# A decoder layer in float32r parts: all first-query-tile scores in parts, and attention inserted in fewer, larger pieces

## The chip, the cores and the metric

The kernel runs on one core of one Trainium2 chip. The metric is device time in microseconds (us) of one execution; three executions of the kernel before took 318.89, 319.07 and 320.75, so its time is the median, 319.07.

## What is computed

One layer for 256 tokens of width 1024. A combined projection gives queries, keys and values for two groups of heads; differential attention (four heads, two softmaxes each, subtracted) and causal attention (eight heads of 64) run on them; an output projection, LayerNorm, a SwiGLU network and a second LayerNorm follow. Cut to what matters:

```
proj = x @ w_in                       # dq dk dv mq mk mv, 512 columns each; rope on q and k
s = q @ k.T * 64**-0.5;  s = where(kpos <= qpos, s, -inf)
a = softmax(s_0) - lam * softmax(s_1)     # group A, 4 heads: 8 score matrices
o_A = rmsnorm(a @ v) * g * (1 - lambda_init)
o_B = softmax(s) @ v                      # group B, 8 heads (256 tokens are one block)
x = layer_norm(ALPHA * x + concat(o_A, o_B) @ w_o)
x = layer_norm(ALPHA * x + (silu(x @ w_g) * (x @ w_u)) @ w_f2)
```

## The kernel before, in words

All weights arrive in units of 128 x 4 x 512 float32 (`raw`). Each unit is split exactly into two float32r parts: `hi` is a cast on ScalarE (L96), `lo` is `raw - hi` on VectorE (L98), with one piece in four of the units 2 to 9 on GpSimd. A product is then three matmuls, hi*hi + hi*lo + lo*hi (`mm3`, L131 to L134). Ring buffers hold five raw units and four of each part.

The input projection has six chunks of 512 columns. Chunks 0 to 3 are q and k of group A, then q and k of group B, each transposed (`proj_qkT`, 32 steps of three matmuls of 256 columns); chunks 4 and 5 are the values of both groups (`proj_v`, 16 steps of three matmuls of 512 columns). Attention is woven in: a table says at which step of which chunk a piece of attention stands in TensorE's program (L38 to L40). `rope` takes a finished block of q or k out of PSUM: a shuffle (`sh`) and a product (`a`) on VectorE, a product on GpSimd, then `finish`: the sum (`a`, L241), a cast to `h` (L243, ScalarE), `l = a - h` (L244, VectorE), and `f` (L245, ScalarE), the first 128 tokens in plain float32.

`scores(g, j)` (L258) makes the scores of two heads: per head three float32r matmuls for query tile 1 (128 queries, 256 keys) from `h` and `l`, and one plain float32 matmul for query tile 0 (128 keys) from `f`. VectorE then adds the mask and takes the row minimum of the negated scores (L271, two instructions per head, each with a read of its accumulator), and ScalarE takes the exponential with its row sum (L274). The score tiles, the transposes of P and the PV products share a PSUM pool of four buffers (`psB`); a tile can be written when the reader of the tile four allocations earlier is done.

For group A, `diff_combine` (L288) subtracts the second softmax from the first on VectorE, after the last exponential of the group; `diff_pt(h)` (L299) transposes the result of one head (three 128x128 transposes, `ppd`, L279 to L281). For group B, `norm1` (L444) and `moba_norm` scale P and `moba_pt` transposes it (`ppm`). `diff_pv` and `moba_pv` multiply by V, and the output projection `wo` follows.

Which instruction of an engine stands where is decided by a list scheduler of the framework from these insertion steps; every engine then runs its own list strictly in order, except that TensorE may load weights ahead.

Of the kernel before, what the change touches and what calls it, by code (L numbers as in the profile page):

```python
# [11 lines left out]
F32 = mybir.dt.float32  # L12
# [18 lines left out]
WARM = 7  # matmuls on zeros that raise the tensor engine's clock while the first loads run  # L31

# weight units loaded / split in more pieces than usual: unit -> pieces
# [3 lines left out]
# steps of a projection chunk at which attention work is woven in  # L37
FIN0, FIN1, FIN2, FIN3 = (20, 24, 28, 31), (4, 6, 8, 10), (5, 4), (5, 2)  # L38
SCORES0, SCORES1 = (18, 22, 26, 30), (3, 5, 7, 9)
COMBINE, DIFF_PT = 12, (22, 25, 28, 31)  # L40

# partner of each rotary dim within a 32-partition quadrant
# [3 lines left out]
# The 256 tokens are one key block of the block-sparse group: there is no past block to select, so  # L46
# its softmax runs over the own block under the causal mask.
# Weight products: every float32 operand is split exactly into two float32r parts (12 bits each), and
# hi*hi + hi*lo + lo*hi accumulate in PSUM.
# [3 lines left out]
def hybrid_layer_kernel(ctx, tc, xT, xr, w_in, w_o, w_f1, w_f2, cols, rows, lamb, rot, tri, out):  # L53
# [11 lines left out]
    # unit: [128, 4 blocks, 512] float32, split into two float32r parts  # L65
# [39 lines left out]
    def spread(units_, pieces, steps):  # L105
        """Hooks that emit the split of some units evenly over a number of steps."""
# [101 lines left out]
    apool = axT.enter_context(tc.tile_pool(name="apool", bufs=1))  # L208
    V = [apool.tile([P, 2, 512], F32, name=f"V{i}") for i in range(2)]
    # per pair of 128-row blocks: first token tile in float32, the rest in two float32r parts  # L210
    F0, QH, QL, SH, QA = {}, {}, {}, {}, {}

    def qk_tiles(c, b):
        kind = c % 2
        n = S if kind else P
        F0[c, b] = apool.tile([P, 2, P], F32, tag=f"f{kind}{b}", name=f"f{c}_{b}")
        QH[c, b] = apool.tile([P, 2, n], F32R, tag=f"h{kind}{b}", name=f"h{c}_{b}")
        QL[c, b] = apool.tile([P, 2, n], F32R, tag=f"l{kind}{b}", name=f"l{c}_{b}")
# [7 lines left out]
    def rope(c, js, ps):  # L226
        """128-row blocks js of q^T or k^T, PSUM -> SBUF, with the rotary part applied."""
# [10 lines left out]
        f, h, l = F0[c, b][:, bs, :], QH[c, b][:, bs, :], QL[c, b][:, bs, :]  # L238

        def finish():  # L240
            nc.vector.tensor_add(a, a, sh)  # L241
            src = a if c % 2 else a[:, :, P:]
            nc.scalar.copy(h, src)  # L243
            nc.vector.tensor_sub(l, src, h.bitcast(F32))  # L244
            nc.scalar.copy(f, a[:, :, :P])  # L245
# [12 lines left out]
    def scores(g, j):  # L258
        b, i = divmod(j, 2)
        cq, ck = 2 * g, 2 * g + 1  # L260
        pr = [psB.tile([P, 3 * P], F32, tag="b", name=f"s{g}_{j}_{s}") for s in range(2)]
        for s in range(2):
            r = slice(64 * s, 64 * s + 64)
            mm3(pr[s][:, :S], QH[cq, b][r, i, :], QL[cq, b][r, i, :], QH[ck, b][r, i, :], QL[ck, b][r, i, :], True, True)
        for s in range(2):
            r = slice(64 * s, 64 * s + 64)
            nc.tensor.matmul(pr[s][:, S:], F0[cq, b][r, i, :], F0[ck, b][r, i, :], start=True, stop=True)
        for s in range(2):
            u = 2 * j + s
            for i, (e, p, m) in enumerate(((E0[g][:, u, :], pr[s][:, S:], mask[:, P:]), (E1[g][:, u, :], pr[s][:, :S], mask))):  # L270
                nc.vector.tensor_tensor_reduce(  # L271
                    out=e, in0=p, in1=m, scale=-0.125, scalar=3.4e38, op0=ALU.add, op1=ALU.min,
                    accum_out=negm[g][:, i, u : u + 1])
                nc.scalar.activation(e, e, AF.Exp, bias=negm[g][:, i, u : u + 1], scale=-1.0,  # L274
                                     accum_out=ls[g][:, i, u : u + 1])
# [12 lines left out]
    def diff_combine():  # L288
        """E_c0 - lam * (l0 / l1) * E_c1, per query row."""
# [84 lines left out]
    def proj_qkT(c, side):  # L374
        """One 512-column chunk, transposed: 128 columns on the partitions, 256 tokens."""
# [29 lines left out]
    def proj_v(c, side):  # L405
        """One 512-column chunk for both token tiles."""
# [18 lines left out]
    for j in range(4):  # L425
        sc.setdefault(SCORES0[j], []).append(lambda j=j: scores(0, j))
# [3 lines left out]
    for h in range(4):  # L430
        sc.setdefault(DIFF_PT[h], []).append(lambda h=h: diff_pt(h))
# [3 lines left out]
    for j in range(4):  # L435
        sc.setdefault(SCORES1[j], []).append(lambda j=j: scores(1, j))
# [11 lines left out]
    for n, u in enumerate(range(6)):  # L448
        sd.setdefault(8 + n, []).append(lambda u=u: moba_pt(u))
    proj_v(5, sd)  # L450

# [93 lines left out]
    ahead(15)  # L545
    mp.close()

# [1 line left out]
    hp = ctx.enter_context(tc.tile_pool(name="hp", bufs=1))  # L549
    hTh = hp.tile([P, NF, S], F32R, name="hTh")  # L550
    hTl = hp.tile([P, NF, S], F32R, name="hTl")
# [176 lines left out]
```

## Time and profile before

| | us | of the span |
|---|---|---|
| time, median of three | 319.07 | |
| span of the profiled execution | 317.0 | |
| TensorE (PE) busy | 304.6 | 96% |
| TensorE weight loads (PEld) busy | 259.7 | 82% |
| VectorE (DVE) busy | 224.4 | 71% |
| ScalarE (ACT) busy | 169.0 | 53% |
| GpSimd (POOL) busy | 36.1 | 11% |
| granted TensorE clock, mean | 0.993 | |

The profiled execution's own time inside the records is its span, 317.0 us; the median of the timed runs is 2.07 us more. The shares are means over stages with different limits: attention is woven into the first third only, and the last two thirds are the feed-forward network, in which TensorE runs without a gap. In the trace a matmul's start is the useful number: ends are modelled, so neighbours overlap, and the distance between starts is what a matmul costs.

### The profile page before, as it was taken

What the parts mean: (1) busy time and instruction counts of PE and PEld (TensorE: products, weight loads), DVE (VectorE), ACT (ScalarE), POOL (GpSimd) and SP (SyncE); (2) the same over time, 40 slices, a digit from 0 to 9 for tenths busy, and PEclk for the clock granted to TensorE, in tenths of its full rate; (3) what the DMA queues carried; (4) which work ended last, traced back from release to release, by engine and by line L of the source; (5) the groups of instructions that cost most, each with busy time, mean ns of one, the idle gap of its engine ahead of it and who ended that gap; (6) DMA issues with size and microseconds to landing.
All of it is one profiled execution on the core that took longest, in us unless ns stands there. A gap on an engine that the chain in (4) does not pass through costs nothing.

```text
span 317.0 us, 4689 instructions
## 1 busy us (share of the span) xinstructions
PE 304.6 (96%) x1741; PEld 259.7 (82%) x1741; DVE 224.4 (71%) x437; ACT 169.0 (53%) x349; POOL 36.1 (11%) x38
## 2 busy tenths in 40 slices
PE   7999899999999999999999999999999999999990
PEld 4999789867887788888888888888888888888880
DVE  3799999999977389949386577658657753343275
ACT  3757489398685328247467547646754642422000
POOL 1076553310030010100000000000000000000011
PEclk9999999999999999999999999999999999999997
DMA  6999963444376442659654574475357474000011
GB/s 176 377 305 375 423 236 134 132 135 147 125 254 213 188 136 74 212 247 309 220 172 142 218 254 136 142 267 167 141 224 254 144 266 132 0 2 0 0 66 67
DMA packets 12310, 57.18 MB, mean 180 GB/s; under 512 B 1504, under 2 KB 2272, under 8 KB 6784
## 3 DMA queue, kind: packets, MB, share of 16 engines
q1 hardware_dynamic: 12000, 54.79, 49.5%
q0 software_dynamic: 288, 2.10, 1.9%
q8 instruction: 13, 0.21, 0.3%
q14 instruction: 9, 0.07, 0.1%
HBM read 55.84 MB, written 1.05 MB: 179 GB/s over the span
## 4 chain that ended last, share of the span: by engine, by line
PE 77%; DVE 12%; DMA 4%; issue 3%; POOL 1%; ACT 1%; SPq 1%; DVEq 0%; ACTq 0%
PE fc L590 21%; PE fc L591 11%; PE fo L134 6%; PE fo L132 6%; PE fo L133 6%; DMA raw<-in_w_in_dram 4%; DVE lo L98 4%; PE wo L132 2%; PE fr L133 2%; PE fr L132 2%; PE wo L134 2%; PE wo L133 2%; PE fr L134 2%; PE pj L132 2%; PE pj L134 2%
## 5 line engine op out<-in xcount | busy, mean ns | idle before, releaser
L98 DVE TENSOR_TENSOR lo<-raw,hi 128x1024 fp32r<-128x1024 f32 (+1 forms) x122 | 118.2, 995 | 41.2 <-ACT hi L96 41.1
L96 ACT CAST hi<-raw 128x512 fp32r<-128x512 f32 (+1 forms) x130 | 100.5, 824 | 38.3 <-PE fo L134 19.2
L590 PE MATMUL fc<-x1T,hi 128*128 128x512 f32 x288 | 100.1, 392 | 0.0
L591 PE MATMUL fc<-x1T,lo 128*128 128x256 f32 x288 | 80.7, 280 | 0.0
L590 PEld LDWEIGHTS fc<-x1T,hi 128*128 128x128 f32 x288 | 54.1, 188 | 11.8
L591 PEld LDWEIGHTS fc<-x1T,lo 128*128 128x128 f32 x288 | 54.1, 188 | 0.0
L132 PE MATMUL pj<-xTh,hi 128*128 128x256 f32 x128 | 37.1, 296 | 1.0 <-DVE xTh L168 0.9
L134 PE MATMUL pj<-xTh,lo 128*128 128x256 f32 x128 | 36.2, 289 | 0.7 <-DVE lo L98 0.5
L133 PE MATMUL pj<-xTl,hi 128*128 128x256 f32 x128 | 36.6, 287 | 0.0
L132 PE MATMUL fo<-hi,hTh 128*128 128x512 f32 x82 | 32.4, 395 | 0.0
L133 PE MATMUL fo<-lo,hTh 128*128 128x512 f32 x82 | 32.4, 395 | 0.0
L134 PE MATMUL fo<-hi,hTl 128*128 128x512 f32 x82 | 32.4, 395 | 0.0
L132 PEld LDWEIGHTS pj<-xTh,hi 128*128 128x128 f32 x128 | 24.6, 195 | 2.6 <-ACT hi L180 2.1
L134 PEld LDWEIGHTS pj<-xTh,lo 128*128 128x128 f32 x128 | 24.4, 194 | 1.3 <-DVE lo L98 0.7
L594 DVE TENSOR_TENSOR v<-v,fc 128x256 f32<-128x256 f32 x36 | 15.0, 418 | 14.5 <-ACT v L593 14.5
L133 PEld LDWEIGHTS pj<-xTl,hi 128*128 128x128 f32 x128 | 25.0, 195 | 0.0
L593 ACT COPY v<-fc 128x256 f32<-128x256 f32 x36 | 13.3, 370 | 20.8 <-PE fc L591 20.7
L505 POOL TENSOR_TENSOR rsf<-rsf,mhalf 128x1 f32<-128x1 f32 x2 | 1.8, 924 | 179.3 <-DVE rsf L504 179.3
L134 PEld LDWEIGHTS fo<-hi,hTl 128*128 128x128 f32 x82 | 15.5, 189 | 3.6
L133 PEld LDWEIGHTS fo<-lo,hTh 128*128 128x128 f32 x82 | 15.5, 189 | 3.6
L132 PEld LDWEIGHTS fo<-hi,hTh 128*128 128x128 f32 x82 | 15.5, 189 | 3.5
L98 POOL TENSOR_TENSOR lo<-raw,hi 128x512 fp32r<-128x512 f32 x8 | 13.5, 1689 | 21.3 <-ACT hi L96 21.3
(148 smaller groups left out, 455.8 us busy)
## 6 DMA issues: line engine op xcount, KB each, us to landing
raw<-in_w_f_dram SPq DMA_DIRECT2D x33, 1024.0 KB, 5.2
raw<-in_w_in_dram SPq DMA_DIRECT2D x24, 256.0 KB, 5.4
raw<-in_w_in_dram SPq DMA_DIRECT2D x4, 1024.0 KB, 10.1
raw<-in_w_o_dram SPq DMA_DIRECT2D x4, 1024.0 KB, 4.8
raw<-in_w_in_dram SPq DMA_DIRECT2D x4, 512.0 KB, 7.9
rows<-in_rows_dram POOLq DMA_DIRECT2D x2, 1024.0 KB, 6.9
x_sb<-in_xr_dram SPq DMA_DIRECT2D x1, 1024.0 KB, 10.5
out_dram<-z SPq DMA_DIRECT2D x3, 256.0 KB, 2.1
```

Source lines behind the costliest of these rows:

```text
L96: nc.scalar.copy(h[:, s, :], r[:, s, :])
L98: eng.tensor_sub(l[:, s, :], r[:, s, :], h[:, s, :].bitcast(F32))
L132: nc.tensor.matmul(ps, sh, mh, start=first, stop=False)
L133: nc.tensor.matmul(ps, sh, ml, start=False, stop=False)
L134: nc.tensor.matmul(ps, sl, mh, start=False, stop=last)
L505: nc.gpsimd.tensor_tensor(rs, rs, mhalf[:, :1], op=ALU.pow)
L590: nc.tensor.matmul(ps, hi[u][:, i, ws], x1T[:, k], start=k == 0, stop=False)
L591: nc.tensor.matmul(ps[:, 0, :], lo[u][:, i, ws], x1T[:, k, 0, :], start=False, stop=k == KT - 1)
L593: nc.scalar.copy(v, ps[:, 1, :])
L594: nc.vector.tensor_add(v, v, ps[:, 0, :])
```

## The change

Six things change together.

- `rope` no longer makes `f`; `h` and `l` of the queries cover all 256 tokens instead of the last 128 (keys had all 256 already).
- Query tile 0's scores are three float32r matmuls of 128 columns from `h` and `l`, like tile 1's, instead of one plain float32 matmul.
- `scores(g, b)` handles four heads, and so takes all four `psB` buffers at once; the two heads of a pair alternate matmul by matmul.
- The insertion steps change from four per group to two: `SCORES0` (18, 22, 26, 30) to (20, 30), `SCORES1` (3, 5, 7, 9) to (5, 11).
- `diff_combine` stands at step 14 of chunk 3 instead of 12, and the transposes of group A at steps 25 and 31, two heads at a time, instead of 22, 25, 28, 31.
- `moba_pt` likewise: two heads at steps 8, 10 and 12 of chunk 5, instead of one at each of 8 to 13.

```diff
-SCORES0, SCORES1 = (18, 22, 26, 30), (3, 5, 7, 9)
-COMBINE, DIFF_PT = 12, (22, 25, 28, 31)
+SCORES0, SCORES1 = (20, 30), (5, 11)
+COMBINE, DIFF_PT = 14, (25, 31)
...
         def finish():
             nc.vector.tensor_add(a, a, sh)
-            src = a if c % 2 else a[:, :, P:]
-            nc.scalar.copy(h, src)
-            nc.vector.tensor_sub(l, src, h.bitcast(F32))
-            nc.scalar.copy(f, a[:, :, :P])
+            nc.scalar.copy(h, a)
+            nc.vector.tensor_sub(l, a, h.bitcast(F32))
...
+    def scores(g, b):
+        cq, ck = 2 * g, 2 * g + 1
+        pr = {}
+        for i in range(2):
+            for s in range(2):
+                pr[i, s] = psB.tile([P, 3 * P], F32, tag="b", name=f"s{g}_{b}_{i}_{s}")
+            for q, o, n in ((slice(P, S), 0, S), (slice(0, P), S, P)):
+                for p, (A, B) in enumerate(((QH, QH), (QL, QH), (QH, QL))):
+                    for s in range(2):
+                        r = slice(64 * s, 64 * s + 64)
+                        nc.tensor.matmul(pr[i, s][:, o : o + n], A[cq, b][r, i, q], B[ck, b][r, i, :n],
+                                         start=p == 0, stop=p == 2)
...
-    for j in range(4):
-        sc.setdefault(SCORES0[j], []).append(lambda j=j: scores(0, j))
+    for b in range(2):
+        sc.setdefault(SCORES0[b], []).append(lambda b=b: scores(0, b))
...
-        sc.setdefault(DIFF_PT[h], []).append(lambda h=h: diff_pt(h))
+        sc.setdefault(DIFF_PT[h // 2], []).append(lambda h=h: diff_pt(h))
...
-    for n, u in enumerate(range(6)):
-        sd.setdefault(8 + n, []).append(lambda u=u: moba_pt(u))
+    for u in range(6):
+        sd.setdefault(8 + 2 * (u // 2), []).append(lambda u=u: moba_pt(u))
```

The scheduler reorders VectorE's list as well. The first place is ahead of group A's combine, in chunk 3 (`lo` with `raw`, `hi`: a weight piece; `sc`: the combine's factors; `E`: the exponentials that it combines). Before:

```order
L271 ISA negm_516 128x1
L235 STREAM_SHUFFLE sh_1_744<-pj_1_520 128x512
L236 TENSOR_TENSOR a_1_745<-pj_1_520,cs_sb 128x512
L98 TENSOR_TENSOR lo_754<-raw_521,hi_753 128x512
L241 TENSOR_TENSOR a_1_745<-a_1_745,sh_1_744 128x512
L291 RECIPROCAL rl_518<-ls_517 128x16
L292 TENSOR_TENSOR sc<-ls_517,rl_518 128x8
L98 TENSOR_TENSOR lo_754<-raw_521,hi_753 128x512
L244 TENSOR_TENSOR l_1_743<-a_1_745,h_1_742 128x256
L293 TENSOR_SCALAR sc<-sc,nlam 128x8
L98 TENSOR_TENSOR lo_754<-raw_521,hi_753 128x512
L296 SCALAR_TENSOR_TENSOR E_514<-E_514,sc 128x128
```

The same place now:

```order
L272 ISA negm_508 128x1
L233 STREAM_SHUFFLE sh_1_745<-pj_1_512 128x512
L234 TENSOR_TENSOR a_1_746<-pj_1_512,cs_sb 128x512
L98 TENSOR_TENSOR lo_822<-raw_596,hi_821 128x512
L239 TENSOR_TENSOR a_1_746<-a_1_746,sh_1_745 128x512
L292 RECIPROCAL rl_510<-ls_509 128x16
L98 TENSOR_TENSOR lo_822<-raw_596,hi_821 128x512
L293 TENSOR_TENSOR sc<-ls_509,rl_510 128x8
L98 TENSOR_TENSOR lo_822<-raw_596,hi_821 128x512
L241 TENSOR_TENSOR l_1_744<-a_1_746,h_1_743 128x512
L294 TENSOR_SCALAR sc<-sc,nlam 128x8
L297 SCALAR_TENSOR_TENSOR E_506<-E_506,sc 128x128
```

The count of `lo` rows shown is three in both, but they are of unit 8 before and of unit 9 now: unit 8's three stand further up now, between the score reductions, so that three more `lo` pieces of VectorE's come before the combine in all; and `l` has 512 columns instead of 256.

The second place is on VectorE from group B's first finished key block (`l_0`) to its first score reduction (`E` with `s`), chunks 3 and 4. Before:

```order
L244 TENSOR_TENSOR l_0_833<-a_0_835,h_0_832 128x512
L235 STREAM_SHUFFLE sh_1_926<-pj_1_750 128x512
L236 TENSOR_TENSOR a_1_927<-pj_1_750,cs_sb 128x512
L98 TENSOR_TENSOR lo_941<-raw_751,hi_940 128x512
L241 TENSOR_TENSOR a_1_927<-a_1_927,sh_1_926 128x512
L98 TENSOR_TENSOR lo_941<-raw_751,hi_940 128x512
L271 ISA E_931,negm_933<-s_0_0_959,mask 128x128
```

The same stretch now:

```order
L239 TENSOR_TENSOR a_0_834<-a_0_834,sh_0_833 128x512
L241 TENSOR_TENSOR l_0_832<-a_0_834,h_0_831 128x512
L98 TENSOR_TENSOR lo_938<-raw_752,hi_937 128x512 x3
L233 STREAM_SHUFFLE sh_1_923<-pj_1_751 128x512
L234 TENSOR_TENSOR a_1_924<-pj_1_751,cs_sb 128x512
L98 TENSOR_TENSOR lo_938<-raw_752,hi_937 128x512
L239 TENSOR_TENSOR a_1_924<-a_1_924,sh_1_923 128x512
L98 TENSOR_TENSOR lo_1016<-raw_838,hi_1015 128x512 x2
L241 TENSOR_TENSOR l_1_922<-a_1_924,h_1_921 128x512
L98 TENSOR_TENSOR lo_1016<-raw_838,hi_1015 128x512 x2
L272 ISA E_928,negm_930<-s_0_0_0_963,mask 128x128
```

Over the whole list up to that first reduction there are five more `lo` pieces than before, and one more `l` (the second key block's, which stood behind the first head's reductions). `l_0` now stands directly behind the sum `a_0` from which ScalarE makes its `h`.

## Rows read from the trace of the kernel before

**Rows 1.** Stretches: length, busy PE, PEld, DVE, ACT, POOL, then clock, DMA, GB/s.
```profile
50.00:66.00 16.00, 15.05 (x118) 13.79 (x117) 15.97 (x31) 10.40 (x28) 5.75 (x4) 1.00 0.39 124
66.00:80.00 14.00, 13.95 (x78) 10.46 (x77) 13.54 (x49) 12.92 (x44) 1.30 (x1) 1.00 0.45 159
80.00:100.00 20.00, 20.00 (x120) 16.59 (x119) 17.76 (x36) 13.64 (x34) 2.79 (x2) 1.00 0.55 188
```

**Rows 2.** Chain of waits around 57 us: start, us, what.
```profile
54.43 0.60 DVE lo L98
...
57.84 0.33 PE ppd L280
58.28 0.12 PE pj L132
```

**Rows 3.** Timeline of TensorE, one insertion of scores: start, us, engine, line, operation.
```profile
41.38 0.28 PE L134 MATMUL pj<-xTh,lo 128*128 128x256 f32 x1
41.59 0.39 PE L132 MATMUL s<-h,h 64*128 64x256 f32 x2
...
42.05 0.39 PE L267 MATMUL s<-f,f 64*128 64x128 f32 x4
42.37 0.39 PE L132 MATMUL pj<-xTh,hi 128*128 128x256 f32 x1
42.59 0.28 PE L133 MATMUL pj<-xTl,hi 128*128 128x256 f32 x1
```

**Rows 4.** Timeline of TensorE's weight loads in that insertion.
```profile
41.59 0.19 PEld L132 LDWEIGHTS s<-h,h 64*128 64x128 f32 x2
41.70 0.20 PEld L133 LDWEIGHTS s<-l,h 64*128 64x128 f32 x2
```

**Rows 5.** Instructions grouped by line and form: busy, mean ns, idle before.
```profile
L244 DVE TENSOR_TENSOR l<-a,h 128x256 fp32r<-128x256 f32 x6 | 2.3, 414 | 0.0
...
L244 DVE TENSOR_TENSOR l<-a,h 128x512 fp32r<-128x512 f32 x2 | 1.4, 677 | 0.0
L243 ACT CAST h<-a 128x512 fp32r<-128x512 f32 x2 | 1.2, 624 | 2.5 <-DVE a L241 2.5
...
L244 DVE TENSOR_TENSOR l<-a,h 128x128 fp32r<-128x128 f32 x4 | 1.0, 278 | 0.0
```

**Rows 6.** Timeline of TensorE in chunk 4, and at `wo`.
```profile
64.27 0.39 PE L133 MATMUL pj<-lo,xTh 128*128 128x512 f32 x1
64.50 0.40 PE L134 MATMUL pj<-hi,xTl 128*128 128x512 f32 x1
...
74.53 0.40 PE L133 MATMUL pj<-lo,xTh 128*128 128x512 f32 x1
...
96.33 0.39 PE L134 MATMUL wo<-hi,mixl 128*128 128x512 f32 x1
```

**Rows 7.** Timeline of VectorE: score reductions, combine, second group, `mixl`.
```profile
43.19 0.27 DVE L271 CUSTOM_DVE_ANT_0 E<-s,mask 128x128 f32<-128x128 f32 x1
...
43.74 0.28 DVE L271 CUSTOM_DVE_ANT_0 E<-s,mask 128x128 f32<-128x128 f32 x1
...
56.02 3.73 DVE L296 SCALAR_TENSOR_TENSOR E<-E,sc 128x128 f32<-128x128 f32 x8
...
69.20 0.28 DVE L271 CUSTOM_DVE_ANT_0 E<-s,mask 128x128 f32<-128x128 f32 x1
...
78.36 0.25 DVE L444 RECIPROCAL rl<-ls 128x16 f32<-128x16 f32 x1 [0.43 <-ACT E L274]
...
94.09 0.74 DVE L333 SCALAR_TENSOR_TENSOR mixl<-dm,gsub,mixh 128x512 fp32r<-128x512 f32 x1
```

**Rows 8.** Timeline of ScalarE: the exponentials of one head, and the next head's first.
```profile
50.33 0.39 ACT L274 ACTIVATE E<-E,negm 128x128 f32<-128x128 f32 x1
...
51.20 0.39 ACT L274 ACTIVATE E<-E,negm 128x128 f32<-128x128 f32 x1
```

**Rows 9.** A stretch behind the last matmul, columns as in Rows 1.
```profile
311.00:313.00 2.00, 0.00 (x0) 0.00 (x0) 2.00 (x5) 0.00 (x0) 0.46 (x1) 0.90 0.00 0
```

More of the change, by code (lines that the diff above doesn't have):

```diff
@@ L209, in hybrid_layer_kernel @@
     V = [apool.tile([P, 2, 512], F32, name=f"V{i}") for i in range(2)]
-    F0, QH, QL, SH, QA = {}, {}, {}, {}, {}
+    QH, QL, SH, QA = {}, {}, {}, {}
     def qk_tiles(c, b):
         kind = c % 2
[L215 to L218, printed above, removed]
+        QH[c, b] = apool.tile([P, 2, S], F32R, tag=f"h{kind}{b}", name=f"h{c}_{b}")
+        QL[c, b] = apool.tile([P, 2, S], F32R, tag=f"l{kind}{b}", name=f"l{c}_{b}")
     epool = axT.enter_context(tc.tile_pool(name="epool", bufs=1))
@@ L237, in rope @@
         nc.gpsimd.tensor_mul(sh, sh, sin2[:, :m, :])
-        f, h, l = F0[c, b][:, bs, :], QH[c, b][:, bs, :], QL[c, b][:, bs, :]
+        h, l = QH[c, b][:, bs, :], QL[c, b][:, bs, :]
         def finish():
             nc.vector.tensor_add(a, a, sh)
-            src = a if c % 2 else a[:, :, P:]
-            nc.scalar.copy(h, src)
-            nc.vector.tensor_sub(l, src, h.bitcast(F32))
-            nc.scalar.copy(f, a[:, :, :P])
+            nc.scalar.copy(h, a)
+            nc.vector.tensor_sub(l, a, h.bitcast(F32))
         return finish
@@ L256, in alloc_group @@
         rl[g] = small.tile([P, 2, 8], F32, tag="rl", name=f"rl{g}")
-    def scores(g, j):
-        b, i = divmod(j, 2)
+    def scores(g, b):
         cq, ck = 2 * g, 2 * g + 1
[L261 to L275, printed above, removed]
+        pr = {}
[8 more added lines that the diff above has]
+                                         start=p == 0, stop=p == 2)
+        for i in range(2):
+            for s in range(2):
+                u = 4 * b + 2 * i + s
+                for t, (e, p, m) in enumerate(((E0[g][:, u, :], pr[i, s][:, S:], mask[:, P:]),
+                                               (E1[g][:, u, :], pr[i, s][:, :S], mask))):
+                    nc.vector.tensor_tensor_reduce(
+                        out=e, in0=p, in1=m, scale=-0.125, scalar=3.4e38, op0=ALU.add, op1=ALU.min,
+                        accum_out=negm[g][:, t, u : u + 1])
+                    nc.scalar.activation(e, e, AF.Exp, bias=negm[g][:, t, u : u + 1], scale=-1.0,
+                                         accum_out=ls[g][:, t, u : u + 1])
@@ L434, in hybrid_layer_kernel @@
     sc = {FIN3[1]: fin}
-    for j in range(4):
-        sc.setdefault(SCORES1[j], []).append(lambda j=j: scores(1, j))
+    for b in range(2):
+        sc.setdefault(SCORES1[b], []).append(lambda b=b: scores(1, b))
     proj_v(4, sc)
```

## The prediction

> **What bounds the kernel now.** Read the stretches first [rows 1]: from 80 us on TensorE is busy in every microsecond (20.00 of 20.00, and so on to the end of the feed-forward network), so a delay of TensorE that is there at 80 us is still there at the end. Before 66 us VectorE has no room: 15.97 of 16.00 us busy from 50 to 66, 13.54 of 14.00 from 66 to 80. Then the chain of waits [rows 2]: up to 57.84 us it runs through VectorE (weight pieces, the combine of group A), and at 57.84 it passes to TensorE, at the second transpose of the first head, which needs the combined exponentials; from there it is TensorE's matmuls. So two questions decide: when will VectorE have combined the first head, and what does TensorE lose or gain between there and the end of the second group's scores.
>
> **An insertion of scores on TensorE.** Where it met no wait, the last projection matmul ahead started at 41.38 and the second one behind at 42.59 [rows 3]. Two projection matmuls at 0.12 each [rows 2] would have taken 0.24 of these 1.21 us, so an insertion for two heads costs 0.97. Its weight loads start 0.11 apart for both heads at once [rows 4]; five such slots (three of 256 columns, two of the plain float32 matmul) are 0.55, and the other 0.42 is the change from the full array to half the rows and back.
>
> After, a pair of heads has six slots, three of them with 128 columns. Their price isn't in the trace: no float32r matmul here has fewer than 256 columns. It is not below half the 0.12 of 256 columns, 0.06; and it could be as much as the plain float32 product of the same columns took, two instructions per head from 42.05 to 42.37 [rows 3], 0.32, less about 0.10 for the change back, 0.22. I take 0.11, because weight loads never start closer, so that a shorter matmul waits for the next load. An insertion of four heads is then 0.42 + 12 x 0.11 = 1.74.
>
> The Trainium skill (TensorE: Matmul & The Clock Gate, Back-to-back issue gap) gives about 81 ns per matmul of 128 columns with its load, in a stream. By that figure an insertion would cost an estimated 0.42 + 6 x 0.11 + 6 x 0.08 = 1.56, and the sum below would be lower by 3 x 0.03 = 0.1 us, since only the last three slots of one insertion lie on its path. No run here shows such a matmul yet.
>
> Group B's four insertions before, with their waits: from 64.50 to 74.53 [rows 6], 10.03 us, of which 20 projection matmuls at 0.23 [rows 6] are 4.62; so 5.41. Two new ones without a wait are 3.48. That is a gain of 1.93 for TensorE, if nothing else waits.
>
> Transposes two heads at a time: the six transposes cost the same; ScalarE's twelve copies remain. I cost this at nothing, between a gain of 0.1 and a loss of 0.1 for each joined pair (the 0.10 at a change of insertion above). The `f` copies that go were ScalarE's and not on the chain; what they give back there is in the waits below.
>
> **VectorE up to the combine.** The same list, plus: four `l` of 128 columns become 256, 4 x (414 - 278) ns = 0.54 us, and two of 256 become 512, 2 x (677 - 414) = 0.53 [rows 5]; together 1.07. Three more weight pieces now stand ahead of the combine, at 0.60 each [rows 2]: 1.80. VectorE was full, so the first head's combine is done 2.87 later: 57.84 becomes 60.71. What covers this on TensorE: the transposes stand three steps later, 9 matmuls, 9 x 0.12 = 1.08 us of work that moves from behind the wait to ahead of it. And the second head's transposes now follow at once: VectorE needs (59.75 - 57.84) / 3 = 0.64 per further head (59.75 is the end of the eight combines that start at 56.02 [rows 7]), TensorE needs only the two transposes left, 0.22; a wait of 0.4. The matmul that started at 64.50 starts at 64.50 + 2.87 - 1.08 + 0.4 = 66.69, **2.2 later**. What TensorE saves in group A's insertions (before 57 us) only makes it wait longer here.
>
> **Group B's scores.** Without new waits 2.2 - 1.93 = 0.3 would be left. But four heads take all four `psB` buffers, and the second insertion can't begin its last pair until VectorE has reduced the fourth head of the first. VectorE's first reduction of this group was at 69.20 [rows 7]. Ahead of it come now the 1.07, the second key block's `l` (0.68), and five weight pieces (3.00): 74.0. At 0.55 per head (43.19 to 43.74 [rows 7]) the fourth buffer is free at 76.2; six slots (0.66) and the change back (half the 0.42, 0.2) bring the matmul behind it to 77.0. Before, step 11 started five matmuls behind 74.53, at 75.69. So this wait leaves **1.3**, not 0.3.
>
> To that come pauses of VectorE that the old list hid. `l_0` stands directly behind the sum, and waits for ScalarE's cast, 0.62 [rows 5]; before, weight pieces lay between. In group A the fifth head's reductions stand behind pieces of unit 8, whose casts now queue behind four heads of exponentials: ScalarE needs 0.87 per head (50.33 to 51.20 [rows 8]), VectorE 0.55, so after four heads ScalarE is 4 x 0.32 = 1.3 late, which two ready pieces (1.2) nearly cover, but not the cast behind them, about 0.5. With GpSimd's part of `rope`, which the new list also has closer behind, these are between 0 and 2.0 us; I take half, 1.0, since some were there before in other places.
>
> **Sum.** 317.0 + 1.3 + 1.0 = 319.3 us of span. The median of the runs is 2.07 above the span, so **321.4 us**.
>
> **Behind it.** After group B's scores ScalarE has 16 heads' halves, 8 x 0.87 = 7.0 us of exponentials, in one run, and VectorE waits for the last before the reciprocal: from 75.2 (74.0, half a head, the 1.0) to 82.2 instead of 78.36 [rows 7], 3.8 later. From there to `mixl`, done at 94.83 [rows 7], VectorE has the same work as before, and TensorE took `mixl` at 96.33 [rows 6], 1.5 later. 3.8 - 1.5 is 2.3, exactly the delay already counted; so this costs nothing in the sum, and what is worse than the sum ahead of it comes out here one for one.
>
> **Bounds.** Low: VectorE's work up to the reciprocal is 1.07 more whatever the order, it had at most the 0.46 of pauses [rows 1] to fill, and TensorE has 1.5 of slack at `mixl`; so the best is 1.07 - 1.5 = -0.4, 318.7 us. High: all the pauses (2.0) and the dear matmul (3 x 0.11) are 1.3 + 2.0 + 0.3 = 3.6, 322.7 us.
>
> **Rivals.**
> - *The weight pieces moved, but TensorE takes the slack.* VectorE's list is the same length in the end (the pieces that come earlier are missing later), so if the pauses stay out and the 1.5 at `mixl` takes up the rest, the shift is -0.4 to 1.2: 318.7 to 320.3, middle 319.4. Against it: the fourth buffer at 76.2, which is counted without any pause. Chance 0.24.
> - *Slower by over 1%.* The place is the first pair of transposes. TensorE arrives there, by the buffers of group A, some 2 to 3 us ahead of VectorE. If that idle time is long enough for the granted clock to fall to 1.2 GHz, the projection behind it runs at half speed; four microseconds of it cost 2, and the time is 321.4 + 2 = 323.4. All pauses together give 322.7 without it. It decides from 0.9 us above the sum. For it: behind the last matmul, with TensorE quite idle, the mean is down to 0.90 from 311 to 313 [rows 9], so idleness does lower it; against it: here TensorE is busy up to the wait and right behind it. Chance 0.25, both mechanisms.
>   The Trainium skill (TensorE: Matmul & The Clock Gate, Part 1) says that half rate is the state to which idleness brings the array back, and activity releases it; the trace agrees [rows 9], and this rule speaks against joining waits into one long one.
> - *Faster by over 1%.* The waits inside the eight old insertions and the changes of array shape go and nothing replaces them: group B's 1.93, and as much again in group A, 3.9; 317.0 - 3.9 + 2.07 = 315.2. It needs VectorE to have room before 57 us, where it has 0.03 of 16 us [rows 1]. Chance 0.03.
>
> **How the numbers follow.** The forecast (shift 1.3 to 3.1, 320.4 to 322.2) has the remaining 0.48. About 1% (3.2 us) is what a measurement of this kernel tells from no change; 322.26 is that line. Faster 0.03; the forecast and the first rival, 0.72, are within 1% except for the forecast's last edge, 0.03: same 0.69; slower 0.28. The range leaves out the faster case, the lowest part of the first rival and the clock case's far end: 318.8 to 323.6.
>
> **What would show it.** In the changed profile: the first transpose of group A released by the combine at 60 to 62 us, with one idle time of 2 to 4 us ahead of it on TensorE; the first reduction of group B at 74 to 76; the reciprocal behind it waiting for an exponential; weight loads of the 128-column scores 0.11 apart; and the last third of the program shifted as a whole. It would be wrong if TensorE's wait at the transposes is under 1 us (VectorE had room after all), or if the clock falls there.

## The result, and the profile after

The changed kernel takes 324.66 us (median of four, 324.42 to 324.92); the kernel before, run beside it, 319.91. The ratio is 1.0164, 95% interval 1.0128 to 1.0200: slower by 1.6%, and 1.06 us above the upper end of the range. The span of the profiled execution is 322.6 us, 5.6 more than before, and the median is again 2.06 above the span. In some executions the granted clock falls to 0.50 between 10 and 16 us, which costs about 1.5 us: the profiled ones of e4, e10 and e13 show it, and of the four times of the kernel before, two (320.75, 320.87) lie about that much above the others (318.89, 319.07), so the 5.6 us between the spans say more of the change than the 4.75 between the medians.

The stretches of the changed kernel, columns as in [rows 1]:

```profile
42.00:44.00 2.00, 1.90 (x13) 1.79 (x14) 2.00 (x7) 1.16 (x3) 0.00 (x0) 0.60 0.65 270
...
60.00:62.00 2.00, 0.10 (x1) 0.00 (x0) 2.00 (x5) 0.62 (x1) 0.16 (x1) 1.00 0.00 0
62.00:64.00 2.00, 0.72 (x3) 0.51 (x4) 1.97 (x7) 0.00 (x0) 0.00 (x0) 0.72 0.34 74
64.00:66.00 2.00, 2.00 (x11) 1.84 (x10) 2.00 (x7) 0.96 (x2) 0.00 (x0) 0.50 1.00 426
...
50.00:66.00 16.00, 12.82 (x99) 12.18 (x97) 15.02 (x41) 9.94 (x31) 4.22 (x3) 0.90 0.54 195
66.00:80.00 14.00, 13.49 (x93) 11.01 (x92) 12.36 (x32) 7.94 (x21) 2.59 (x2) 0.99 0.30 95
```

TensorE is idle for 3 us around 60 to 63, and behind it the clock is at 0.50, the lower of its two levels. VectorE, which had 0.03 us of room from 50 to 66 and 0.46 from 66 to 80 [rows 1], now has 0.98 and 1.64: its milestones come later although it is less busy, so it waits. Where it waits, and when its milestones come, is in its timeline:

```profile
35.52 0.91 DVE L241 TENSOR_TENSOR l<-a,h 128x256 fp32r<-128x256 f32 x1
38.94 1.49 DVE L239 TENSOR_TENSOR a<-a,sh 128x256 f32<-128x256 f32 x1
...
46.04 0.69 DVE L239 TENSOR_TENSOR a<-a,sh 128x512 f32<-128x512 f32 x1 [0.69 <-POOL sh L235]
...
51.14 0.69 DVE L98 TENSOR_TENSOR lo<-raw,hi 128x512 fp32r<-128x512 f32 x1 [0.59 <-ACT hi L96]
52.18 1.36 DVE L98 TENSOR_TENSOR lo<-raw,hi 128x512 fp32r<-128x512 f32 x1 [0.35 <-ACT hi L96]
...
62.87 1.41 DVE L297 SCALAR_TENSOR_TENSOR E<-E,sc 128x128 f32<-128x128 f32 x4
...
67.72 0.69 DVE L239 TENSOR_TENSOR a<-a,sh 128x512 f32<-128x512 f32 x1 [0.90 <-POOL sh L235]
69.15 0.69 DVE L241 TENSOR_TENSOR l<-a,h 128x512 fp32r<-128x512 f32 x1 [0.74 <-ACT h L240]
...
77.84 0.28 DVE L272 CUSTOM_DVE_ANT_0 E<-s,mask 128x128 f32<-128x128 f32 x1
...
85.38 0.25 DVE L445 RECIPROCAL rl<-ls 128x16 f32<-128x16 f32 x1 [2.43 <-ACT E L275]
...
101.14 0.74 DVE L334 SCALAR_TENSOR_TENSOR mixl<-dm,gsub,mixh 128x512 fp32r<-128x512 f32 x1
```

Against [rows 7]: the combine starts at 62.87 instead of 56.02, group B's first reduction at 77.84 instead of 69.20 (8.64 later), the reciprocal at 85.38 instead of 78.36, `mixl` at 101.14 instead of 94.09. TensorE's timeline at the same places:

```profile
63.28 0.47 PE L280 MATMUL ppd<-ident,E 128*128 128x128 f32 x1 [3.18 <-DVE E L297]
...
71.90 0.40 PE L134 MATMUL pj<-hi,xTl 128*128 128x512 f32 x1
...
72.69 0.23 PE L265 MATMUL s<-h,h 64*128 64x128 f32 x2
72.75 0.28 PE L265 MATMUL s<-h,l 64*128 64x128 f32 x2
72.86 0.29 PE L265 MATMUL s<-l,h 64*128 64x128 f32 x2
72.97 0.34 PE L265 MATMUL s<-h,h 64*128 64x256 f32 x2
...
73.76 0.50 PE L132 MATMUL pj<-hi,xTh 128*128 128x512 f32 x1
...
77.81 0.40 PE L134 MATMUL pj<-hi,xTl 128*128 128x512 f32 x1
78.61 0.84 PE L265 MATMUL s<-h,h 64*128 64x256 f32 x2 [0.40 <-DVE negm L272]
...
81.02 0.50 PE L132 MATMUL pj<-hi,xTh 128*128 128x512 f32 x1
...
101.93 0.50 PE L134 MATMUL wo<-hi,mixl 128*128 128x512 f32 x1
```

Group B's first insertion meets no wait: 73.76 - 71.90 - 0.23 = 1.63 us for four heads (0.23 is one projection matmul [rows 6]). The second takes 81.02 - 77.81 - 0.23 = 2.98, because each score buffer waits for VectorE's reductions (`negm`). The projection behind it, step 11, started at 75.69 before, five matmuls behind the 74.53 of [rows 6]; now it starts at 81.02, 5.3 later, and `wo` with `mixl` at 101.93 instead of 96.33 [rows 6], 5.6 later, which is also what the span lost.

### The profile page after: what moved, and what is told of

The parts are those of the page before. It is cut to its first block, busy times and chain, and to the rows that moved or that the text cites. A ratio compares the mean times of both kernels' runs of the same rounds, so it can differ in the third digit from the quotient of the medians.

```text
span 322.6 us, 4703 instructions
## 1 busy us (share of the span) xinstructions
PE 305.3 (95%) x1757; PEld 260.7 (81%) x1757; DVE 226.2 (70%) x437; ACT 167.1 (52%) x337; POOL 33.6 (10%) x38
## 4 chain that ended last, share of the span: by engine, by line
PE 74%; DVE 13%; DMA 5%; issue 3%; ACT 2%; SPq 2%; POOL 0%; DVEq 0%; ACTq 0%; POOLq 0%
PE fc L591 20%; PE fc L592 10%; PE fo L133 6%; PE fo L134 6%; PE fo L132 6%; DMA raw<-in_w_in_dram 5%; DVE lo L98 3%; DVE a L239 2%; PE wo L132 2%; PE wo L134 2%; PE fr L132 2%; PE fr L133 2%; PE wo L133 2%; PE fr L134 2%; PE pj L132 2%
## 5 line engine op out<-in xcount | busy, mean ns | idle before, releaser
L275 ACT ACTIVATE E<-E,negm 128x128 f32<-128x128 f32 (+1 forms) x32 | 14.1, 443 | 6.0 <-DVE negm L272 6.0
```

The costliest lines, as they stand in the source:

```text
L275: nc.scalar.activation(e, e, AF.Exp, bias=negm[g][:, t, u : u + 1], scale=-1.0, accum_out=ls[g][:, t, u : u + 1])
```

## The experiments

The names of the expectations: V, W and C are VectorE's work and order with the regrouping, the wider `l`, and the falling clock; O is the order of VectorE's list, A the float32r products themselves, K the clock behind a wait.

**Halving the change.** e1 is the arithmetic alone in the kernel before; e2 the insertions, steps and joined transposes alone, with the old product from `f`.

```diff
 e1, in scores(g, j), two heads per insertion
-            nc.tensor.matmul(pr[s][:, S:], F0[cq, b][r, i, :], F0[ck, b][r, i, :], start=True, stop=True)
+            mm3(pr[s][:, S:], QH[cq, b][r, i, :P], QL[cq, b][r, i, :P], QH[ck, b][r, i, :P], QL[ck, b][r, i, :P], True, True)
 e2
-SCORES0, SCORES1 = (18, 22, 26, 30), (3, 5, 7, 9)
-COMBINE, DIFF_PT = 12, (22, 25, 28, 31)
+SCORES0, SCORES1 = (20, 30), (5, 11)
+COMBINE, DIFF_PT = 14, (25, 31)
```

> Only the arithmetic of the change: no f, h and l of the queries over all 256 tokens, query tile 0's scores as three float32r matmuls; insertions of two heads, steps, combine and transposes as before. Theory V (VectorE's work and order carry the loss, and nearly all of it comes with the regrouping, which puts the exponentials' reductions in blocks and lets pieces and sums collide with GpSimd): 1.07 us more on VectorE at least, so 320 to 322 us. Rival W (the wider l carries it, since l was seen at 0.85 to 1.51 us instead of 0.41 where GpSimd runs): 323 to 325 us. Rival C (two falls of the granted clock to 1.2 GHz carry it, each behind a wait that the four-head insertion or the joined transposes made): no fall here, so 319.5 to 321.

> Only the regrouping: scores of four heads in one insertion with the old plain float32 product for query tile 0 (f kept, narrow h and l of the queries), the new insertion steps, combine at 14, transposes two heads at a time. Theory V: most of the loss, 322 to 324 us, with the first reduction of group B later than 75 us. Rival W: little, 319.5 to 321. Rival C: the two waits and the two falls of the clock are there (stretches around 40 and 62 us below 0.9), 323 to 325 us.

e1 took 325.19 us, ratio 1.0215 (1.0188 to 1.0243); e2 took 319.79, ratio 1.0027 (1.0010 to 1.0045). So the loss comes with the arithmetic, and the regrouping, which I had looked at most, costs 0.9 us by itself. Theory V's guess, that the regrouping brings it, is wrong. VectorE in e1, with a wait for a cast of unit 8:

```profile
52.64 0.69 DVE L98 TENSOR_TENSOR lo<-raw,hi 128x512 fp32r<-128x512 f32 x1 [1.55 <-ACT hi L96]
...
75.92 0.28 DVE L267 CUSTOM_DVE_ANT_0 E<-s,mask 128x128 f32<-128x128 f32 x1
```

The first reduction of group B is at 75.92 with the old insertions, and at 71.81 in e2, whose row is this:

```profile
71.81 0.28 DVE L277 CUSTOM_DVE_ANT_0 E<-s,mask 128x128 f32<-128x128 f32 x1
```

But in e1 that reduction is not where TensorE waits last. Here is TensorE in e1: the first transpose, then the projection matmuls ahead of group B's first insertion and behind it, and a stretch of 2 us:

```profile
62.97 0.33 PE L275 MATMUL ppd<-ident,E 128*128 128x128 f32 x1 [3.89 <-DVE E L292]
...
71.58 0.40 PE L134 MATMUL pj<-hi,xTl 128*128 128x512 f32 x1
...
72.75 0.50 PE L132 MATMUL pj<-hi,xTh 128*128 128x512 f32 x1
```

```profile
64.00:66.00 2.00, 2.00 (x12) 2.00 (x11) 2.00 (x7) 0.48 (x1) 0.00 (x0) 0.50 0.71 291
```

and the same first transpose in the kernel before, with an insertion there that met no wait:

```profile
57.45 0.33 PE L279 MATMUL ppd<-ident,E 128*128 128x128 f32 x1 [0.62 <-DVE E L296]
...
73.08 0.40 PE L134 MATMUL pj<-hi,xTl 128*128 128x512 f32 x1
...
74.19 0.50 PE L132 MATMUL pj<-hi,xTh 128*128 128x512 f32 x1
```

TensorE waits 3.89 us for the combine and is 5.52 late there (62.97 against 57.45). With the clock at 0.50 behind it, the same steps up to group B's first insertion take 8.61 us (71.58 - 62.97) instead of 7.05 (64.50 [rows 6] - 57.45): 1.56 more. Group B's insertions behind it (1.17, 1.17, 1.53 and 1.17 between the two projection matmuls of each) hold hardly a wait that could swallow it. So in e1 the late combine and the fall of the clock behind it make the loss: 7.1 us, of which those insertions give 0.85 back, since they wait less than before. An insertion without a wait is 1.17 in e1 and 1.11 before (the two rows at 73.08 and 74.19).

**The width of `l`, and the clock.** e4 gives VectorE the old `l`; e3 keeps TensorE busy at the first transposes.

```diff
 e4, in finish and scores, cut
-            nc.scalar.copy(h, a)
...
+            src = a if c % 2 else a[:, :, P:]
+            nc.scalar.copy(h, src)
...
-            for q, o, n in ((slice(P, S), 0, S), (slice(0, P), S, P)):
+            for q, o, n in ((slice(0, P), 0, S), (slice(0, P), S, P)):
 e3, ahead of the first transpose of head 0
+        if name == "d0":
+            for _ in range(18):
+                nc.tensor.matmul(ps[:, :, :], warm[:, :P], warm[:, : 3 * P], start=True, stop=True)
```

> The changed kernel with h and l of the queries for the last 128 tokens only; query tile 0's matmuls take the same operands (so the scores of the first 128 tokens are those of the wrong queries: this part of the computation is changed). TensorE's work is that of the changed kernel, VectorE's l is that of the kernel before. Theory V: 1.07 us of plain work goes, and the order stays bad: 323 to 324. Rival W: nearly all of the loss goes, 320 to 321. Rival C: 324 to 325.

> The changed kernel with 18 matmuls on zeros (384 columns, bfloat16) ahead of the first transpose of group A, into the tile that the transposes then overwrite, so that TensorE isn't idle while it waits for the combine; VectorE's list is the same. Theory V and rival W: the clock stays up there, but VectorE is as late as before, so the time is that of the changed kernel within 0.5 us, 324.2 to 325.2. Rival C: the projection behind the transposes runs at full speed; 13 starts of 0.213 become 0.118, so 1.2 us come back: 323.4.

e4 took 325.16 us (ratio 1.0203, 1.0180 to 1.0226), so rival W, that nearly all of the loss goes with the width, falls. What the width itself costs, e4 doesn't say: its list on VectorE isn't quite the changed kernel's, and its first reduction of group B, at 78.63, is at 77.1 less the 1.5 us that its profiled execution lost at the start, 0.7 ahead of the changed kernel's 77.84. e3 took 326.09 (1.0253, 1.0190 to 1.0317). Its stretches:

```profile
60.00:62.00 2.00, 2.00 (x14) 1.21 (x13) 2.00 (x6) 0.62 (x1) 0.00 (x0) 1.00 0.00 0
...
82.00:84.00 2.00, 2.00 (x6) 1.56 (x5) 0.87 (x6) 2.00 (x11) 0.00 (x0) 0.50 0.05 21
```

and the first reduction of group B on VectorE, and the end of the second insertion on TensorE:

```profile
77.75 0.28 DVE L272 CUSTOM_DVE_ANT_0 E<-s,mask 128x128 f32<-128x128 f32 x1
```

```profile
80.94 0.50 PE L132 MATMUL pj<-hi,xTh 128*128 128x512 f32 x1
```

The clock stayed at 1.00 at the transposes, and group B's second insertion still ended at 80.94 (81.02 in the changed kernel), because VectorE's reduction was where it was, 77.75 (77.84). The speed that TensorE kept there only made it arrive earlier at the next wait, and the clock fell behind that one instead. Behind it no wait follows, and there the fall does cost: from 80.94 to `wo` with `mixl` (103.21) e3 takes 22.27 us, the changed kernel 20.91 (101.93 - 81.02), which is the 1.3 us that e3's span is longer. So the fall at 62 to 66 us costs the changed kernel nothing, and rival C falls for that place in that kernel (in e1, where no later wait follows, the fall at the same place cost 1.56).

**The order of VectorE's list.** e5 is the changed kernel, e6 is e1, both with the same constraint: unit 8's pieces are issued behind group A's last reduction, unit 9's behind the combine, as before the change. No instruction is added or taken away. e9 is e6 with the narrow `l` of e4.

```diff
+    MARK, HOLD = {}, {8: 'red0', 9: 'comb'}
...
+            k = HOLD.get(u)
+            if eng is nc.vector and k in MARK:
+                with tc.issue_after(MARK[k].ins):
+                    eng.tensor_sub(l[:, s, :], r[:, s, :], h[:, s, :].bitcast(F32))
```

> The changed kernel with one thing forced: on VectorE, unit 8's lo pieces are issued behind the last score reduction of group A, and unit 9's behind the last instruction of the combine, as in the kernel before (29 pieces ahead of the combine instead of 32, 26 ahead of the last reduction instead of 29). Theory O (the scheduler's new order on VectorE carries the loss): last reduction of group A near 52 instead of 55.9, combine from about 58.5 instead of 62.9, first reduction of group B near 74 instead of 77.8; 320 to 322 us. Rival A (the float32r products themselves, with the insertion's waits, carry it): no change from the changed kernel, 324 to 326.

> The kernel with the arithmetic alone changed (two-head insertions, 325.2 us), and VectorE's pieces of units 8 and 9 held back in the same way (26 ahead of group A's last reduction instead of 28, 29 ahead of the combine instead of 32). Theory O: most of the 6 us comes back, 320 to 322 us. Rival A: 324 to 326.

> The kernel with the arithmetic changed and VectorE's pieces held back (322.1 us), with h and l of the queries for the last 128 tokens only; query tile 0's matmuls take the same operands, so the scores of the first 128 tokens are those of the wrong queries. TensorE's work is unchanged, VectorE's is that of the kernel before. Theory O+W (order first, then the 1.07 us and more of wider l): the 3 us that are left go, 319 to 320.5. Rival A (the float32r products on TensorE): stays at 321.5 to 322.5.

e6 took 322.11 us (1.0104, 1.0063 to 1.0144) where e1 took 325.19: 3.1 of e1's 6.3 us are the place of a few pieces on VectorE. In the traces TensorE waits 0.96 us at the first transposes instead of 3.89, the clock stays at 1.00 behind them, and the matmul ahead of group B's first insertion starts at 66.25 instead of 71.58; of these 5.3 us 2.1 go again in waits of group B's insertions that e1 didn't meet. e9 took 322.69 (1.0103, 1.0066 to 1.0139), no better than e6, and a little above where rival A had put it: the 3 us that e6 still loses aren't the width. (In the traces e9 is 0.5 ahead of e6 at `wo`; the times can't tell so little.) Rows of VectorE in e6, a pause that is left and the first reduction of group B:

```profile
57.70 0.69 DVE L247 TENSOR_TENSOR l<-a,h 128x512 fp32r<-128x512 f32 x1 [0.90 <-ACT h L246]
...
71.53 0.28 DVE L273 CUSTOM_DVE_ANT_0 E<-s,mask 128x128 f32<-128x128 f32 x1
```

e5 took 323.64 (1.0148, 1.0115 to 1.0181), only 1.0 better than the changed kernel, although its first reduction of group B is 3.35 earlier:

```profile
74.49 0.28 DVE L278 CUSTOM_DVE_ANT_0 E<-s,mask 128x128 f32<-128x128 f32 x1
```

Two things took most of that. Two held pieces now stand between the reductions of group B's second and third head, so the fourth head, whose buffer the second insertion waits for, is done only about 2.1 earlier:

```profile
75.60 1.28 DVE L104 TENSOR_TENSOR lo<-raw,hi 128x512 fp32r<-128x512 f32 x2
```

And the clock falls behind the waits of the second insertion:

```profile
78.00:80.00 2.00, 1.95 (x12) 1.78 (x13) 2.00 (x12) 2.00 (x11) 0.00 (x0) 0.54 0.92 266
80.00:82.00 2.00, 2.00 (x7) 1.59 (x6) 0.81 (x6) 2.00 (x11) 0.00 (x0) 0.61 0.55 229
```

e10 measures that fall: e5 with ten matmuls on zeros, five ahead of each pair of the second insertion, and the same lists on VectorE and ScalarE.

```diff
+        fill = psA.tile([P, 512], F32, tag="acc", name="fill") if (g, b) == (1, 1) else None
...
+                    nc.tensor.matmul(fill, warm[:, :P], warm, start=True, stop=True)
```

> The changed kernel with VectorE's pieces held back (323.6 us), and ten matmuls on zeros (512 columns, bfloat16, a spare PSUM tile) at the second insertion of group B, five ahead of each pair, where TensorE waits for score buffers; VectorE's and ScalarE's lists are the same. Theory K (the wait there lets the clock fall, and what lies behind runs at 1.2 GHz for about 2 us on the path that sets the end): clock 1.00 from 78 to 84, time 0.9 to 1.4 us less, 322.3 to 322.8. Rival (the reciprocal and mixl, VectorE's work behind the scores, set the end anyway): the time stays within 0.4 us, 323.2 to 324.

```profile
78.00:80.00 2.00, 2.00 (x15) 1.03 (x15) 2.00 (x10) 1.61 (x9) 0.00 (x0) 1.00 0.49 139
80.00:82.00 2.00, 2.00 (x18) 1.67 (x15) 2.00 (x16) 2.00 (x10) 0.00 (x0) 1.00 0.92 328
```

In the records, from the first projection behind the insertion to the same matmul in chunk 5 it is 79.45 to 92.83 in e5, 13.38 us, and 80.46 to 92.87 in e10, 12.41: the fall costs 0.97. The times, 323.06 (1.0122, 1.0089 to 1.0156) against 323.64, go the same way by 0.6, with intervals that overlap. So the clock costs a microsecond or more where it falls behind the last wait (0.97 here, 1.3 in e3, 1.56 in e1), and nothing where it falls ahead of one; the prices are from the traces, the timing doesn't settle them.

**One piece moved, alone.** e13 is the kernel before, with the reductions of group A's last two heads behind the first piece of unit 8.

```diff
+    def late():
+        with tc.issue_after(MARK[8, 0].ins):
+            LATE[0]()
...
+    sc.setdefault(1, []).append(late)
```

> The kernel before, arithmetic and insertions untouched, with one forced change of order on VectorE: the score reductions of group A's last two heads stand behind the first piece of unit 8 (as all kernels with the float32r parts have it by the scheduler's choice). That piece needs ScalarE's hi of unit 8, which needs the buffer that TensorE reads until the last quarter of chunk 2. Theory O: VectorE waits 0.5 to 1.5 us at that piece, the last reduction comes 2 to 4 us later than 49.6, the combine 1.5 to 3 us later than 56.0, and the time is 320 to 322 us. Rival A (the float32r arithmetic carries the loss by itself): 318 to 319.3.

It took 318.66 us, ratio 1.0007 (0.9988 to 1.0025): no change, against theory O as I had put it, and where rival A had put it. The combine and group B's first reduction on VectorE:

```profile
59.14 2.71 DVE L308 SCALAR_TENSOR_TENSOR E<-E,sc 128x128 f32<-128x128 f32 x8
...
70.70 0.28 DVE L273 CUSTOM_DVE_ANT_0 E<-s,mask 128x128 f32<-128x128 f32 x1
```

Less the 1.5 us of the profiled execution's start, the combine is 1.6 later than the 56.02 of [rows 7], and the first reduction of group B, 69.2, where it was. The piece is done anyway before that reduction, only earlier, and no pause was added ahead of it. So the combine may come later without loss, as long as what VectorE must have done before group B's first reduction stays the same and without pauses. It is the sum up to there that counts, and not the order at one place.

**Towards a faster kernel.** Four kernels turn VectorE's list towards TensorE's waits: the combine is written at step 0 of chunk 3, most of the pieces and the `rope` sum come behind it, unit 10's and 11's pieces, written at other steps of chunk 4, behind group B's reductions (e7 from the changed kernel, e8 from e2); e12 and e11 are the same two with work given to ScalarE.

```diff
 e7, e8
-COMBINE, DIFF_PT = 14, (25, 31)
+COMBINE, DIFF_PT = 0, (25, 31)
+    HOLD = {8: "comb", 9: "comb", 10: "red10", 11: "red11"}
...
 e12, e11, on top of these
-                nc.vector.tensor_copy(V[c - 4][:, t, :], pss[t])
+                nc.scalar.copy(V[c - 4][:, t, :], pss[t])
-        nc.vector.tensor_scalar(E0[1][:, u, :], E0[1][:, u, :], rl[1][:, 0, u : u + 1], None, op0=ALU.mult)
+        nc.scalar.activation(E0[1][:, u, :], E0[1][:, u, :], AF.Copy, scale=rl[1][:, 0, u : u + 1])
```

> The changed kernel with VectorE's order turned towards TensorE's waits: combine written at step 0 of chunk 3; behind it on VectorE all but the first piece of unit 8, unit 9 and the rope sum and l of chunk 2's second block; unit 10's pieces behind the first four heads' reductions of group B, unit 11's behind the last. Theory O: transposes don't wait, first reduction of group B near 70, second insertion without a wait for a score buffer, so TensorE gets back the 0.9 at the transposes and group B's 1.93 of before: 315 to 318 us. Rival A: 322 to 325.

> The regrouping alone (old arithmetic, 319.8 us) with the same order on VectorE as in the run before it in this list. Theory O: 315 to 317.5 us, a little better than with the float32r parts, since l is 1.07 us less on VectorE. Rival A: as the regrouping alone, 319 to 320.

> The same two moves to ScalarE in the changed kernel with the early order (322.9 us). Theory V: mixl near 96 instead of 98.5, so the 3.7 us of wait and slow clock at the output projection go: 319 to 320.5 us, the rest being the wait at the first insertion of group A and the wider l. Rival: 321.5 to 323.

> The regrouping alone with VectorE's order turned towards TensorE's waits (321.2 us), and 3.0 us of VectorE's work ahead of mixl given to ScalarE: the copies of V out of PSUM, and the scaling of P for query tile 0 (eight of 128 columns). Theory V (VectorE's total work up to mixl is what ends last): mixl 2 to 3 us earlier than 96.2, TensorE keeps the 1.56 us that it was ahead at the output projection, and the clock doesn't fall there: 316.8 to 318 us. Rival (ScalarE becomes the bound behind the exponentials): 319.5 to 322.

e7 took 322.86 us (1.0118, 1.0078 to 1.0158) and e8 321.17 (1.0061, 1.0026 to 1.0096), both far from what I expected: TensorE got through group B's scores earlier (the second insertion of e8 ended 1.65 ahead of the kernel before), and then waited at `wo` for `mixl`, which the pieces put behind the reductions had made late (1.82 us in e7, 2.06 in e8). With 3 us of VectorE's work ahead of `mixl` on ScalarE, e11 took 317.44 (0.9954, 0.9936 to 0.9973) and e12 320.95 (1.0065, 1.0041 to 1.0088). That is 3.7 us from two lines in e11, and 1.9 in e12: VectorE's work is what ends last, at `mixl` too.

e14 and e15 add one edit to e11 and e12: the sum of `rope` in chunk 2, which in e11 made VectorE wait 0.98 us for GpSimd between the two reductions of the first head, stands behind the reductions of four heads (and is written one step later).

```diff
-FIN0, FIN1, FIN2, FIN3 = (20, 24, 28, 31), (4, 6, 8, 10), (5, 4), (5, 2)
+FIN0, FIN1, FIN2, FIN3 = (20, 24, 28, 31), (4, 6, 8, 10), (6, 4), (5, 2)
...
-            if c == 2 and js[-1] == 3:
-                with tc.issue_after(MARK["comb"].ins):
+            if c == 2:
+                with tc.issue_after(MARK["comb" if js[-1] == 3 else "red00"].ins):
```

> The kernel of 317.4 us (regrouping alone, VectorE's early order, 3 us given to ScalarE) with the rope sum of chunk 2's first block issued behind the first four heads' reductions, so that VectorE doesn't wait 0.98 us for GpSimd between the first head's two reductions while TensorE waits for a score buffer. Theory K: TensorE's wait of 1.5 + 0.5 us at the second insertion of group A and the fall of the clock behind it (46 to 53 us at 0.50 to 0.67, 2.3 us) go, TensorE is at the first transposes near 57 instead of 60.4, and the time falls by 1 to 2 us more: 315.5 to 316.5. Rival (VectorE's list up to mixl ends last there too, so TensorE only waits later): 316.8 to 317.8.

> The same for the changed kernel (early order and the two moves to ScalarE, 321.0 us): rope sum of chunk 2's first block behind the first four reductions. Theory K: group A's first insertion still waits for its operands and the clock falls there once, so it gains less: 319.5 to 320.7. Rival: within 0.3 us of 321.0.

e14 took 315.28 us, ratio 0.9905 (0.9882 to 0.9929): the fastest kernel of the study, 0.95% under the kernel before and, by the two ratios (0.9905 and 1.0164), 2.5% under the changed one. e15 took 320.63 (1.0058, 1.0036 to 1.0079), the same as e12 within the intervals. e14's first transpose and `wo` on TensorE, and group B's first reduction and `mixl` on VectorE:

```profile
56.03 0.27 PE L299 MATMUL ppd<-ident,E 128*128 128x128 f32 x1
...
93.10 0.39 PE L141 MATMUL wo<-hi,mixl 128*128 128x512 f32 x1
```

```profile
68.71 0.28 DVE L291 CUSTOM_DVE_ANT_0 E<-s,mask 128x128 f32<-128x128 f32 x1
...
91.09 0.74 DVE L353 SCALAR_TENSOR_TENSOR mixl<-dm,gsub,mixh 128x512 fp32r<-128x512 f32 x1
```

The transposes don't wait (no releaser in the row), the reduction is 0.5 earlier than before, `mixl` 3.0 earlier and `wo` 3.2 earlier. How much of the 0.95% is the regrouping's isn't shown: no run has the turned list and the two moves to ScalarE with the old insertions. With the same constraints and moves the kernel with the float32r parts takes 320.63 against 315.28 (spans of the profiled executions 317.0 and 313.6, e15's being its fastest); the scheduler's lists in the two aren't the same, so this is not the price of the parts alone.

## Why the prediction was wrong

- **The chain was right.** Group B's first reduction is late, the second insertion waits for score buffers, and what is lost there stays to the end: the shift of step 11 (5.3), of `wo` (5.6) and of the span (5.6) agree. The slack at `mixl` too: the reciprocal waits 2.43 us for an exponential, VectorE is 7.05 later at `mixl`, TensorE 5.6, and the difference is the 1.5 of the text.
- **The step that failed is the term "pauses of VectorE that the old list hid"**: between 0 and 2.0, of which I took 1.0. The five waits in the rows above are 0.69 + 0.59 + 0.35 + 0.90 + 0.74 = 3.27 us ahead of group B's first reduction, where the kernel before has 0.1 from 40 us to its first reduction. I had priced only one of them well, `l_0` behind ScalarE's cast (0.62 foreseen, 0.74). The two waits for GpSimd's part of `rope`, 1.59 together, went into half a sentence, and the cast of unit 8, 0.94, I put at 0.5. The upper bound was therefore not a bound: it left out that a sum now stands directly behind its shuffle and product, with GpSimd's product (1.29 at 66.40) between them.
- **The wider `l` was counted at its quiet price.** 1.07 us is right where GpSimd is quiet, but between 35 and 41 us `l` took 0.91 instead of 0.41 and a sum 1.49 instead of 0.41 (what such a sum takes at 39.74 in the kernel before) beside GpSimd; the first reduction of group A was 1.87 us later than before (45.06 against 43.19), where the count gives 0.54 for the four `l`: up to there the `l` rows add to 5.26 us instead of 2.16, and other rows and waits are 1.2 less. The kernel before has such collisions too (a `lo` of 1.49 at 51.16), so only a part is new.
- **The ledger of the first reduction:** 69.20 + 4.75 (1.07, 0.68, 3.00, as counted) + 3.27 (waits) = 77.2, and 77.84 was measured; the 0.6 left are the collisions, net of those that the kernel before had elsewhere: the `l` rows are 4.2 more where 1.75 were counted, but the combine takes 2.72 instead of 3.73, one factor `sc` 0.15 instead of 0.98. Predicted was 74.0 + 1.0 = 75.0. The 2.8 us between, 2.3 of them the pauses, are the whole miss but for 0.5: the span came out 3.3 above the 319.3 of the sum.
- **The clock rival was right in its mechanism and wrong in its price.** The idle time at the first transposes was 3.18 us, in the 2 to 4 that were named, and the clock fell to 0.50 behind it. The Trainium skill (TensorE: Matmul & The Clock Gate, Part 1) has idleness as what takes the rate away, and the trace agrees. But e3 shows that in the changed kernel this fall is not on the path. The text named it as a sign of being wrong; the sign came, the time came out in the rival's region, and the cause was another.
- **TensorE's prices held.** The four-head insertion was put at 1.74 and took 1.63. Its weight loads stay 0.11 apart, as said (that loads "never start closer" was too much: those of two transposes start 0.06 apart at 57.84 in the kernel before); the matmuls of 128 columns start 0.06, 0.11 and 0.11 apart, 0.28 for three, under the 0.33 of the sum. The Trainium skill's 81 ns (TensorE: Matmul & The Clock Gate, Back-to-back issue gap) would make it 0.24. Neither moved the result.
- **Said of the first transposes:** released at 60 to 62; it was 63.28. **Of the last third:** shifted as a whole; it was, by 5.6 to 5.7.
- **Which half of the change:** the prediction put the loss on the second insertion of four heads. e1 and e2 show that the arithmetic alone costs 6.3 us and the regrouping 0.9 (6.2 and 0.9 by the spans). Together they cost less than the sum, 5.6 by the spans. The traces give a likely reason: e1 pays 1.56 for the clock behind the transposes, and in the changed kernel a later wait swallows that fall. The intervals of e1 and of the changed kernel just overlap, so the times alone don't settle it.
- **What stays open.** That the arithmetic acts through VectorE's list is shown for about half of e1's loss by e6 (3.1 us from order alone), and for the changed kernel by e5 (group B's first reduction 3.35 earlier, though only 1.0 us of time). That rival W's width isn't what carries it is shown by e4 and e9. Rival A, TensorE's products, came close with its times for e9 (321.5 to 322.5) and right for e13 (318 to 319.3), so by the times it isn't refuted for the 3 us that e6 and e9 still lose. The traces speak against it: an insertion of two heads without a wait is 0.06 longer in e1 (1.17 against 1.11), 0.5 for all eight, and in e9 TensorE still waits 2.19 us for VectorE (`negm`) in group B's third insertion, at 72.92. Which entries of the list make up the 3 us is only read from e6's trace (the 0.90 and 0.43 us waits for ScalarE's casts, and collisions ahead of 44 us) and was not tried one by one; e13 shows that one such entry by itself can be free. Why the scheduler orders so is not told by any run here: its model of durations is not in a trace.

## What to carry to other kernels

When an edit changes durations that a list scheduler reads, the list of the engine that has no room is the change; read it row by row, and give each row that now directly follows its producer on another engine that producer's whole duration as a wait, not a share. Find the last point at which the two engines meet and add up work, waits and collisions to there; it moves from kernel to kernel (group B's first reduction and `mixl` in the changed kernel, the combine in e1), so look for it anew after each edit. A gain on an engine that then waits is not a gain, and a loss ahead of a wait is not a loss: e3 and e13 show one of each.

## What the runs showed of the hardware

**VectorE and GpSimd block each other in turns.** GpSimd's timeline in the changed kernel, two pieces in a row:

```profile
36.99 3.16 POOL L98 TENSOR_TENSOR lo<-raw,hi 128x512 fp32r<-128x512 f32 x2
```

Beside them VectorE's instructions with two operands in SBUF were long (`a` 1.49, the row at 38.94). In the kernel before it was GpSimd that was held up at this place, and VectorE's `l` kept its pace (0.75 for two of them at 40.68):

```profile
40.14 3.04 POOL L98 TENSOR_TENSOR lo<-raw,hi 128x512 fp32r<-128x512 f32 x1 [2.54 <-ACT hi L96]
```

The Trainium skill (SBUF — State Buffer, Who interferes with whom) says that a VectorE instruction with two inputs in SBUF contends with a GpSimd instruction that reads SBUF, and that issue order decides who blocks. The trace agrees, with 1.49 us for a sum that takes 0.41 undisturbed (at 39.74 in the kernel before), and 3.04 for a GpSimd piece that takes 1.28 at 51.70 in the changed kernel. So the price of a GpSimd piece depends on where VectorE's list stands, and a new order moves it from one engine to the other.

**The clock moves with the wait.** In the kernels shown the clock fell behind a wait, at places that differ (42 and 62 us in the changed kernel, 62 in e1, 82 in e3, 78 in e5). In e3, filling one wait with matmuls on zeros kept it up there, and moved the idle time and the fall to the next wait; in e10, at the last such wait, it kept the clock at 1.00 from 78 to 82.
